# Four Strassen units in the last gate pair, its weights asked for behind x1's last read-back

## The chip, the cores and the metric

The kernel runs on one core of one Trainium2 chip. A core has TensorE (PE in the profile; PEld is its weight load), VectorE (DVE), ScalarE (ACT), GpSimd (POOL) and SyncE (SP), which here issues nearly all transfers between HBM and the on-chip memory. The metric is the device time of one execution in microseconds; the time of a kernel is the median of its runs.

## The reference

One layer of a hybrid decoder trunk for 256 tokens of width 2048. Cut to what matters:

```python
h = rmsnorm(x, norm_mix_g); u = h @ w_in          # split into branches and gates
...                                               
m = sigmoid(ga) * (ya @ w_a_out) + sigmoid(gb) * (yb @ w_b_out)
x = x + m @ w_o
gate = sigmoid(rmsnorm(x, ple_norm_g) @ w_ple_gate)
x = x + gate * (p @ w_ple_proj)
return rmsnorm(x, final_norm_g)
```

All of it is float32. The change lies in the product with `w_ple_gate` (2048 x 2048) and in what surrounds it; the sum `x + m @ w_o` is called x1 below.

## The kernel before

**Products.** Every matrix product with a weight is done as three products of a rounded type (FP32R), because each float32 operand is split into a high part and the rest: high times high, high times rest, rest times high. The weights come from HBM as float32 into one of three buffers of 1 MB each (`raw`, `load_raw`, lines 116 to 134). `split` (line 146) makes the two parts of a weight tile: ScalarE rounds it into `whi` (line 166), and VectorE subtracts that from the weights and writes `wlo` (line 167). These parts lie in ten buffers, six of a pool `late` and four of a pool `wp`, in this stage. TensorE then takes three matmuls per weight chunk of 128 rows and half of the tokens (lines 1269 and 1293).

**Steps, units, groups.** The work is a list `steps`; a group is one block of 512 output columns, or a pair of blocks, over all 2048 rows. Two or four steps make a unit, and a unit is one weight buffer of 1 MB. Most groups run their chunks one after the other (line 1269). A pair group follows a program of eight units (lines 41 to 47): `(0, c)` is a plain unit for the first block, two chunk pairs; `(1, c)` the same for the second; `(2, c)` a plain unit that takes the same rows for both blocks; `("S", c)` is a Strassen unit for one chunk pair c, which computes with 7 products of 128 x 512 what takes 8 (lines 1311 to 1321). A Strassen unit needs sums of weights: after its first split, `combine_weights` (lines 174 to 188) makes them on VectorE in place, with the operations of lines 184, 187 and 188. It has four splits, one of them of half the width, where a plain unit has two. It also needs sums of the other operand: `forms` (line 780) makes four of them, splits them and keeps them as `So0` and `So1`, for x1's first and second quarter.

**The end of the kernel.** The last groups are `w_o`'s blocks 2 and 3, the gate block 0 (`PG`, eight steps, positions `late` to `late + 7`), the gate pair 1 and 2 (`GP`, program `LATE`, from `late + 8` on) and the gate block 3 (the last group, lines 1460 to 1483). The pair's accumulators are eight: four in banks "g", one for each half of the tokens and each block, and four in banks "s" for Strassen products. `sums` (line 859) adds them up when they are complete: a copy on ScalarE (line 868), additions on VectorE (line 855), then the sigmoid (line 1025). The gate times the kept projection `p @ w_ple_proj`, added to x1, are the operations of lines 1028 and 1029 in `gated`; GpSimd multiplies with the final gain (line 1037). The last group runs in three passes, each in a bank: the first half of the tokens over 512 columns, then the second half over twice 256 columns. After each pass come the evictions of `last_half` and the norm.

**What sets the order.** The program is traced in the order of positions, and a scheduler of the compiler fixes each engine's order from that, from what it expects to be ready and from explicit ties: `tc.issue_after(i)` puts what is traced in the block behind instruction `i` on `i`'s engine, without a wait for its end. `step` ties the work after a product behind the splits traced last; `tied` is a list of ranges of positions whose splits are tied one behind the other. `ahead` (line 1257) says how many steps ahead of the products the splits are traced: three at `late`, eight from `late + 17` on. `ask_ahead` (line 1273) traces the weight loads up to two units further.

**Queues around the change.** x1 arrives in quarters of 512 columns. `turned` (line 338) transposes a quarter: four writes to HBM (line 350), one read back (line 354), then a transposition of small blocks on VectorE (line 358); `put` (lines 313 and 314) splits it into `xh` and `xl`. All these transfers, the weights (lines 119, 121, 126, 131) and the reads of the kept projections (`load_projection`, line 1220) stand in one queue of SyncE. The last quarter's transposition falls into the gate block 0, whose last two steps multiply with that quarter. In `load`, the weights of `w_o`'s plain blocks are tied behind the last of the four writes (`state["sent"]`).

Of the kernel before, what the change touches and what calls it, by code (L numbers as in the profile page):

```python
# [23 lines left out]
CW = 512  # L24
# [19 lines left out]
INNER = (0, 4), ("S", 0), (0, 6), ("S", 1), (2, 3), ("S", 2), (1, 4), (1, 6)  # L44
FRONT = (0, 2), (0, 4), (0, 6), ("S", 0), (1, 2), ("S", 1), (1, 4), (1, 6)
OUT = (0, 4), ("S", 0), (1, 4), ("S", 1), (2, 3), ("S", 2), (0, 6), (1, 6)
LATE = (0, 4), ("S", 0), (0, 6), ("S", 1), (2, 3), ("S", 2), (1, 4), (1, 6)


PRM_GMIX, PRM_GPLE, PRM_GHG, PRM_LB, PRM_CONV = 0, 16, 32, 40, 48  # L50
# [5 lines left out]
def hybrid_kernel(ctx, tc, xT, x, pT, prm, gfin, masks, w_in, w_a, w_b, w_o, w_pg, w_pp, out):  # L56
    nc = tc.nc
# [23 lines left out]
    state = {"tmp": "tmp1"}  # L81
# [3 lines left out]
    def nm(s):  # L85
        uid[0] += 1
        return f"{s}_{uid[0]}"

    def t4(tag="t4", bufs=None):
        bufs = bufs or {"tmp1": 8, "tmp2": 4, "tmp3": 5}[state["tmp"]]  # L90
        return pools[state["tmp"]].tile([P, 1024], F32, tag=tag, bufs=bufs, name=nm(tag))

    def bank(tag):
        return ps.tile([P, CW], F32, tag=tag, bufs=4, name=nm(tag))
# [7 lines left out]
    unit_of, part_of, joint, across = [], [], [], []  # L102
    loaded = {}
# [1 line left out]
    half = {}  # L105

    def load(pos):
        if unit_of[pos] not in loaded and groups[steps[pos][0]][0] == "O":
            with tc.issue_after(state["sent"]):
                return load_raw(pos)  # L110
        return load_raw(pos)

    def load_raw(pos):
        w, g, c = stream[pos]
        if unit_of[pos] not in loaded:
            raw = wp.tile([P, 2, 2 * CW], F32, tag="raw", bufs=3, name=nm("raw"))
            loaded[unit_of[pos]] = raw
            if joint[pos]:
                nc.sync.dma_start(out=raw[:, 0, :], in_=w[g, :, c, :])
                for i in range(2):  # L120
                    nc.sync.dma_start(
                        out=raw[:, 1, i * CW : (i + 1) * CW], in_=w[g + 1, :, c, (1 - i) * CW : (2 - i) * CW]
                    )
            elif across[pos]:
                for i in range(2):
                    nc.sync.dma_start(out=raw[:, i, :], in_=w[g + i, :, c, :])
            elif FIRST <= pos < FIRST + 20:
                for i in range(2):
                    nc.sync.dma_start(out=raw[:, i, :], in_=w[g, :, c + i, :])
            elif pos >= FIRST:  # L130
                nc.sync.dma_start(out=raw, in_=w[g, :, c : c + 2, :])
        return loaded[unit_of[pos]]
# [10 lines left out]
    def split(pos, c0=0, c1=2 * CW):  # L143
        part = part_of[pos]
        src = load(pos)[:, part % 2, :]
        if joint[pos]:

            src = load(pos)[:, part == 3, :]
            if part == 1:
                src, c1 = half[unit_of[pos]], CW  # L150

        pool, n = (pools["late"], 6) if (pos - state.get("late", len(steps))) % 10 < 6 and "late" in state else (wp, 4)
        places = [(pool, n, tag) for tag in ("whi", "wlo")]
        n = len(MORE[more(pos)])
        if pos % (4 + n) < n:
            places = [(pools[name], 1 + (tag == "X"), tag) for name, tag in MORE[more(pos)][pos % (4 + n)]]
        if pos not in parts:
            parts[pos] = tuple(
                pool.tile([P, 2 * CW << (tag[:3] == "yaT")], F32R, tag=tag, bufs=n, name=nm("w" + x))[:, : 2 * CW] for (pool, n, tag), x in zip(places, ("hi", "lo"))
            )  # L160
        hi, lo = parts[pos]
        s = slice(c0, c1)
        with ExitStack() as order:
            for i in (*(state["splits"] if more(pos) == "inner" or any(pos in at for at in tied) else ()),):
                order.enter_context(tc.issue_after(i))
            a = nc.scalar.activation(out=hi[:, s], in_=src[:, s], func=AF.Copy)  # L166
            v = nc.vector.tensor_tensor(  # L167
                out=lo[:, s], in0=src[:, s], in1=hi[:, s].bitcast(F32), op=ALU.subtract
            )
        state["splits"] = (a.ins, v.ins)  # L170
        if joint[pos] and part == 0:
            combine_weights(pos)
# [17 lines left out]
    groups = []  # L190
# [13 lines left out]
    groups += [("OO", 0, w_o, 0, "mT", OUT), ("O", 2, w_o, 2, "mT"), ("O", 3, w_o, 3, "mT")]  # L204
    groups += [("PG", 0, w_pg, 0, "x1T"), ("GP", 1, w_pg, 1, "x1T", LATE), ("PG", 3, w_pg, 3, "x1T")]
    steps = []
# [36 lines left out]
    gates, late = of_kind("GG"), of_kind("PG")[0]  # L243
# [6 lines left out]
    tied = []  # L250
# [4 lines left out]
    closing = last_unit("OO", OUT)  # L255
    last = range(gates[-1] + 1, closing + 1)
    outer = range(closing + 6, of_kind("O")[-1] + 1)
    tied.append(range(last[0] - 4, late + 10))
    inner = [of_kind(kind) for kind in ("QV", "VG")]
    inner = range(inner[0][0] - 3, inner[0][-1] + 1), range(inner[1][0] - 6, inner[1][-1] + 1)  # L260

# [79 lines left out]
    def turned(src, lag, dst=None):  # L341

        d = dram.tile([P, 4, T], F32, tag="turn", bufs=3, name=nm("turn"))
        to = d.rearrange("(b i) a x -> a i b x", b=4)
        for a in range(4):
            state["sent"] = nc.sync.dma_start(  # L350
                out=to[a], in_=src[32 * a : 32 * a + 32, :].rearrange("i (b x) -> i b x", b=4)
            ).ins
        yield
        nc.sync.dma_start(out=src, in_=d.rearrange("p a x -> p (a x)"))
        for _ in range(lag):
            yield
        dst = t4() if dst is None else dst
        nc.vector.transpose(
            out=dst.rearrange("p (k a e) -> p a k e", a=4, e=32), in_=src.rearrange("p (a k e) -> p a k e", a=4, e=32)
        )  # L360
        return dst
# [589 lines left out]
    def ep_o(j, psum):  # L951
# [18 lines left out]
        if j < 2:  # L970
# [6 lines left out]
            yield  # L977
            chunks = [c for u, c in LATE if u == "S" and c // 2 == j]
            r = x1.rearrange("p (u k t) -> p u k t", u=2, k=2)[:, : len(chunks)]
# [59 lines left out]
    def last_half(t, h, psum):  # L1039

        xs, pw, ss, n = state["x"], state["pw", 3], state["ss3"], CW // 2
        gt = t4()
        squares, gt = gt[:, : n + (t == 1 and h == 1)], gt[:, :n]
        d = xs[:, t, 3 * CW + h * n : 3 * CW + (h + 1) * n]
        nc.scalar.activation(out=gt, in_=psum, func=AF.Sigmoid, scale=state["rstd2"][:, t : t + 1])
        nc.vector.tensor_tensor(  # L1046
            out=gt, in0=gt, in1=pw[:, t * CW + h * n : t * CW + (h + 1) * n], op=ALU.mult
        )
        nc.vector.tensor_tensor(out=d, in0=d, in1=gt, op=ALU.add)
        if t == 1 and h == 1:  # L1050

            d = state["whole"][:, NT * D - n : NT * D + 1]
        nc.vector.scalar_tensor_tensor(
            out=squares, in0=d, scalar=1.0 / D, in1=d, op0=ALU.mult, op1=ALU.mult,
            accum_out=ss[:, t * 6 + 3 + h : t * 6 + 4 + h],
        )
# [47 lines left out]
    def ep_last(t, halves):  # L1104

        last_half(t, 0, halves[0])
        sums_so_far(t)
        last_half(t, 1, halves[1])
        last_norm(t)
        yield  # L1110
# [106 lines left out]
    def load_projection(j):  # L1217

        pw = state["pw", j] = t4("pw", 2)
        nc.sync.dma_start(out=pw, in_=state["kept", j])  # L1220

    def third_part():

# [25 lines left out]
    def advance():  # L1249
        for e in list(active):  # L1250
            step(e)
# [12 lines left out]
    def product(psum, op, k, t, hi, lo, first, last, which=(0, 1, 2)):  # L1264

        oh, ol = (x[:, k, t * P : (t + 1) * P] for x in op)
        for n in which:
            a, b = ((oh, hi), (oh, lo), (ol, hi))[n]
            m = nc.tensor.matmul(psum, a, b, start=first and n == 0, stop=last and n == 2)  # L1269
            if late + 5 <= pos < late + 12:  # L1270
                tc.keep_in_program_order(m)
# [62 lines left out]
    for pos, (gi, c) in enumerate(steps[:last_group]):  # L1334
# [85 lines left out]
        for i in range(2):  # L1420
            k = 2 * c + i
            for c0, c1 in EARLY[0][:2] if pos == 0 and i == 0 else ((0, CW),):
                s = slice(i * CW + c0, i * CW + c1)
# [35 lines left out]

    nlast = len(steps) - last_group  # L1460
    for t, halves in ((0, (0, 1)), (1, (0,)), (1, (1,))):
        bk, n = bank("g"), CW // 2
        for c in range(nlast):
            if done < len(steps):
                split(done)
                done += 1
            hi, lo = parts[last_group + c]
            for i in range(2):
                k = 2 * c + i
                s = slice(i * CW + halves[0] * n, i * CW + (halves[-1] + 1) * n)  # L1470
                product(bk[:, : len(halves) * n], state["x1T"], k, t, hi[:, s], lo[:, s], k == 0, k == KT - 1)
            if c % 2:
                advance()
        if t == 0:
            active.append(ep_last(t, [bk[:, h * n : (h + 1) * n] for h in halves]))
        else:
            last_half(t, halves[0], bk[:, :n])
            if halves[0] == 0:
                sums_so_far(t)
# [76 lines left out]
```

## Time and profile before

| | us |
|---|---|
| median of 3 runs | 807.52 (807.15 to 807.83) |
| the profiled execution | 807.97 |
| its span, from first to last instruction | 806.2 |
| TensorE busy | 797.0 |
| VectorE busy | 686.9 |
| ScalarE busy | 494.1 |
| GpSimd busy | 89.2 |

The profile is one execution. In a row of a timeline stand the start, the time, the engine, the line of the kernel, the operation, what is written and read, how many are merged, and in brackets the idle time of the engine before the row with what ended it. `SPq` rows are requests of SyncE's queue; their time is that of the request and not of the transfer. A matmul of 512 columns is shown with 0.39 us, but the next one starts 0.227 us later, since matmuls overlap. Likewise one VectorE split of 128 x 1024 is shown with 1.22 us and the next starts 1.14 us later.

### The profile page before, as it was taken

The numbers are of one execution on the slowest core, as the hardware profiler recorded it, in microseconds if no ns is written. First come the engines' busy times: TensorE is split into PE (matmuls) and PEld (weight loads), VectorE is DVE, ScalarE is ACT, GpSimd is POOL, SyncE is SP. The second block draws the span as 40 slices with busy tenths as digits, with TensorE's granted clock in tenths as the row PEclk, the third lists the DMA queues.
The fourth block names the chain that finished last, engine by engine and source line by source line (L and its number), as shares of the span: only waits on it lengthen the run. The fifth ranks groups of instructions, "written<-read, shape, count | busy, mean of one in ns | idle before, by whom it ended". The sixth has DMA issues, their size and how long they took to land.

```text
span 806.2 us, 11109 instructions
## 1 busy us (share of the span) xinstructions
PE 797.0 (99%) x4168; PEld 662.5 (82%) x4169; DVE 686.9 (85%) x794; ACT 494.1 (61%) x666; POOL 89.2 (11%) x74
## 2 busy tenths in 40 slices
PE   9999999999999999999999999999999999999995
PEld 7888888888888888888888888888888888888885
DVE  6969897966778987978998998998998998879894
ACT  7867575575665665586674564564565556765652
POOL 0000145300000054300001000100100000002012
PEclk9999999999999999999999999999999999999998
DMA  9899855747776755668584775775875669987532
GB/s 344 308 322 314 275 169 205 242 167 231 251 262 197 257 179 202 209 206 261 187 310 159 220 277 168 249 260 184 263 274 196 209 240 350 368 268 258 222 120 104
DMA packets 50309, 191.20 MB, mean 237 GB/s; under 512 B 5712, under 2 KB 15184, under 8 KB 36304
## 3 DMA queue, kind: packets, MB, share of 16 engines
q1 hardware_dynamic: 50112, 190.24, 68.7%
q8 instruction: 32, 0.52, 0.3%
q10 hardware_dynamic: 144, 0.26, 0.1%
q14 instruction: 21, 0.17, 0.1%
HBM read 175.80 MB, written 14.68 MB: 236 GB/s over the span
## 4 chain that ended last, share of the span: by engine, by line
PE 93%; DVE 3%; issue 1%; ACT 1%; DMA 1%; POOL 0%; ACTq 0%; POOLq 0%; DVEq 0%
PE g L1269 49%; PE g L1293 30%; PE s L1293 8%; PE s L1269 3%; DVE wlo L167 1%; PE s L514 1%; DMA raw<-in_w_pg 1%; PE s L1142 1%; DVE t L855 0%; DVE t L1028 0%; ACT whi L166 0%; DVE t L1046 0%; DVE xs L1029 0%; PE s L647 0%; PE s L670 0%
## 5 line engine op out<-in xcount | busy, mean ns | idle before, releaser
L167 DVE TENSOR_TENSOR wlo<-raw,whi 128x1024 fp32r<-128x1024 f32 (+1 forms) x320 | 392.2, 1249 | 85.0 <-ACT whi L166 83.6
L166 ACT ACTIVATE whi<-raw 128x1024 fp32r<-128x1024 f32 (+1 forms) x320 | 326.3, 1047 | 167.4 <-PE g L1269 93.4
L1269 PE MATMUL g<-whi,xh 128*128 128x512 f32 (+1 forms) x464 | 177.5, 383 | 0.0
L1269 PE MATMUL g<-whi,xl 128*128 128x512 f32 (+1 forms) x464 | 177.2, 382 | 0.0
L1269 PE MATMUL g<-wlo,xh 128*128 128x512 f32 (+1 forms) x464 | 177.1, 382 | 0.0
L1293 PE MATMUL g<-wlo,xh 128*128 128x512 f32 x316 | 122.9, 389 | 0.0
L1293 PE MATMUL g<-whi,xl 128*128 128x512 f32 x316 | 122.9, 389 | 0.0
L1293 PE MATMUL g<-whi,xh 128*128 128x512 f32 x316 | 122.4, 389 | 0.0
L1269 PEld LDWEIGHTS g<-whi,xh 128*128 128x128 f32 x464 | 87.2, 188 | 17.2 <-ACT xh L313 0.4
L1269 PEld LDWEIGHTS g<-whi,xl 128*128 128x128 f32 x464 | 87.2, 188 | 17.1 <-DVE xl L314 0.2
L1269 PEld LDWEIGHTS g<-wlo,xh 128*128 128x128 f32 x464 | 87.2, 188 | 16.6
L166 ACT ACTIVATE whi<-t 128x512 fp32r<-128x512 f32 x25 | 15.8, 632 | 91.3 <-DVE t L187 86.7
L1293 PEld LDWEIGHTS g<-wlo,xh 128*128 128x128 f32 x316 | 59.3, 188 | 12.4
L1293 PEld LDWEIGHTS g<-whi,xh 128*128 128x128 f32 x316 | 59.3, 188 | 12.3
L1293 PEld LDWEIGHTS g<-whi,xl 128*128 128x128 f32 x316 | 59.3, 188 | 12.2
L184 DVE TENSOR_TENSOR raw<-raw 128x1024 f32<-128x1024 f32 x25 | 31.5, 1262 | 0.7
L937 POOL TENSOR_TENSOR t<-ga,gb 128x512 f32<-128x512 f32 x6 | 10.6, 1788 | 188.0 <-issue 118.1
L1269 PE MATMUL g<-whi,yaTh 128*128 128x512 f32 (+1 forms) x74 | 28.3, 389 | 0.0
L1269 PE MATMUL g<-whi,yaTl 128*128 128x512 f32 (+1 forms) x74 | 28.0, 384 | 0.0
L1269 PE MATMUL g<-wlo,yaTh 128*128 128x512 f32 (+1 forms) x74 | 27.9, 383 | 0.0
L1269 PE MATMUL g<-whi,ybTh 128*128 128x512 f32 x64 | 24.9, 389 | 0.0
L1269 PE MATMUL g<-wlo,ybTh 128*128 128x512 f32 x64 | 24.9, 389 | 0.0
(317 smaller groups left out, 1110.6 us busy)
## 6 DMA issues: line engine op xcount, KB each, us to landing
raw<-in_w_in SPq DMA_DIRECT2D x68, 1024.0 KB, 5.0
raw<-in_w_in SPq DMA_DIRECT2D x37, 512.0 KB, 5.3
raw<-in_w_o SPq DMA_DIRECT2D x12, 1024.0 KB, 5.6
raw<-in_w_pg SPq DMA_DIRECT2D x12, 1024.0 KB, 6.5
raw<-in_w_in SPq DMA_DIRECT2D x38, 256.0 KB, 5.6
turn<-t SPq DMA_DIRECT2D x72, 128.0 KB, 2.8
t<-turn SPq DMA_DIRECT2D x18, 512.0 KB, 5.2
raw<-in_w_a SPq DMA_DIRECT2D x8, 1024.0 KB, 5.6
```

What stands on the lines that cost most here:

```text
L166: a = nc.scalar.activation(out=hi[:, s], in_=src[:, s], func=AF.Copy)
L167: v = nc.vector.tensor_tensor(out=lo[:, s], in0=src[:, s], in1=hi[:, s].bitcast(F32), op=ALU.subtract)
L184: nc.vector.tensor_tensor(out=b[:, 0:4:3, :], in0=b[:, 0:3:2, :], in1=b[:, 3:4, :].to_broadcast([P, 2, CW]), op=ALU.subtract)
L514: nc.tensor.matmul(heads(bk)[r, h, c if at is None else slice(at, at + 32)], key(h)[:, r], query(h)[:, c], start=True, stop=True, tile_pos ...
L937: (nc.vector if j == 3 else nc.gpsimd).tensor_tensor(out=spread(m, t), in0=blocks(ga[:, s]), in1=blocks(gb[:, s]), op=ALU.add)
L1142: nc.tensor.matmul(wb[:m, :n], *ones, start=True, stop=True)
L1269: m = nc.tensor.matmul(psum, a, b, start=first and n == 0, stop=last and n == 2)
L1293: m = nc.tensor.matmul(banks[name], x, y[:, s], start=k == total[name] and i == 0, stop=k == 1 and i == 2)
```

## The change

In the program of the last pair, the plain unit over both blocks for chunk 3 becomes a Strassen unit, and the plain unit of the second block goes ahead of the two Strassen units that now follow each other. The weight loads of the pair, save for its first unit at `late + 8`, are tied behind the read-back traced last, which for them is that of x1's last quarter; so are the reads of the kept projections. The range of tied splits reaches one position further, to the first split of the pair's first Strassen unit. The first pass of the last group takes a bank "s" instead of "g". Since chunk 3 lies in x1's second quarter, `forms` makes operands for two chunks there instead of one (line 978 takes them from `LATE`), and the pair has 24 steps instead of 22.

```diff
-LATE = (0, 4), ("S", 0), (0, 6), ("S", 1), (2, 3), ("S", 2), (1, 4), (1, 6)
+LATE = (0, 4), ("S", 0), (0, 6), ("S", 1), (1, 4), ("S", 2), ("S", 3), (1, 6)
...
     def load(pos):
-        if unit_of[pos] not in loaded and groups[steps[pos][0]][0] == "O":
-            with tc.issue_after(state["sent"]):
+        after = {"O": "sent", "GP": "read"}.get(groups[steps[pos][0]][0])
+        if unit_of[pos] not in loaded and after and pos != late + 8:
+            with tc.issue_after(state[after]):
                 return load_raw(pos)
         return load_raw(pos)
...
-    tied.append(range(last[0] - 4, late + 10))
+    tied.append(range(last[0] - 4, late + 11))
...
-        nc.sync.dma_start(out=src, in_=d.rearrange("p a x -> p (a x)"))
+        state["read"] = nc.sync.dma_start(out=src, in_=d.rearrange("p a x -> p (a x)")).ins
...
         pw = state["pw", j] = t4("pw", 2)
-        nc.sync.dma_start(out=pw, in_=state["kept", j])
+        with tc.issue_after(state["read"]):
+            nc.sync.dma_start(out=pw, in_=state["kept", j])
...
-        bk, n = bank("g"), CW // 2
+        bk, n = bank("g" if t else "s"), CW // 2
```

## Prediction

> **What bounds the kernel now.** I read the page first: TensorE is busy in 99% of the span, and 93% of the chain that ended last is TensorE. Then I read the chain in order of time around the last gate pair, where the change lies.
>
> ```profile
> span 806.2 us, 11109 instructions
> PE 93%; DVE 3%; issue 1%; ACT 1%; DMA 1%; POOL 0%; ACTq 0%; POOLq 0%; DVEq 0%
> ...
> 734.24 5.44 PE g L1293 x24
> ...
> 744.44 5.44 PE g L1293 x24
> ```
>
> A plain unit of the pair is 24 matmuls in 5.44 us, 0.2267 us each. From the first row to the second lie one plain and one Strassen unit, 10.20 us, so a Strassen unit (21 matmuls) takes 4.76. I looked along TensorE for starts further apart than 0.24 us after the opening and the attention products, and found one place:
>
> ```profile
> 728.08 0.39 PE L1269 MATMUL g<-whi,xl 128*128 128x512 f32 x1
> ...
> 729.30 0.40 PE L1269 MATMUL g<-whi,xh 128*128 128x512 f32 x1
> ```
>
> From the first row to the second are four starts, 1.22 us where 0.91 would do: 0.31 us lost, just when the first gate group reaches x1's last quarter. The three windows to the end show who stands next in line:
>
> ```profile
> 740.00:760.00 20.00, 20.00 (x90) 16.57 (x89) 19.23 (x19) 10.92 (x13) 4.77 (x2) 1.00 0.53 183
> 760.00:780.00 20.00, 20.00 (x90) 16.57 (x89) 18.22 (x19) 12.09 (x17) 1.45 (x2) 1.00 0.63 233
> 780.00:806.20 26.20, 18.11 (x126) 16.77 (x124) 15.74 (x37) 6.91 (x14) 5.74 (x6) 0.91 0.21 80
> ```
>
> Columns: length, PE, PEld, DVE, ACT, POOL, clock, DMA. VectorE is busy 19.23 and 18.22 of 20 us. TensorE sets the pace by a thin margin, and the change takes from TensorE and gives to VectorE.
>
> **What the change takes from TensorE.** One plain unit becomes a Strassen unit: three matmuls, 3 x 0.2267 = 0.68 us. The weights of the first Strassen unit are now asked for behind the read-back of x1's last quarter:
>
> ```profile
> 706.07 0.43 SPq L1220 DMA_DIRECT2D pw<-kept  x1
> 714.30 0.33 SPq L131 DMA_DIRECT2D raw<-in_w_pg  x1
> 715.98 2.31 SPq L350 DMA_DIRECT2D turn<-t  x4
> 718.39 0.57 SPq L119 DMA_DIRECT2D raw<-in_w_pg  x1
> 719.01 0.46 SPq L121 DMA_DIRECT2D raw<-in_w_pg  x1
> 721.77 0.33 SPq L354 DMA_DIRECT2D t<-turn  x1
> ...
> 724.89 1.23 DVE L167 TENSOR_TENSOR wlo<-raw,whi 128x1024 fp32r<-128x1024 f32 x1 [1.81 <-ACT whi L166]
> 726.60 1.25 DVE L358 STREAM_TRANSPOSE t<-t 128x1024 f32<-128x1024 f32 x1 [0.48 <-DMA t<-turn]
> 728.42 1.69 DVE L314 SCALAR_TENSOR_TENSOR xl<-t,prm_t,xh 128x256 fp32r<-128x256 f32 x4 [0.58 <-ACT xh L313]
> ...
> 736.62 1.28 DVE L1028 TENSOR_TENSOR t<-t,pw 128x512 f32<-128x512 f32 x2
> ```
>
> The two requests at 718.39 and 719.01 (768 KB) go behind 721.77, so the read-back, 4.8 us in flight today (721.77 to 726.60), finds less in its way. It has to win only 0.31 us to close the gap; bounds 0 and 0.31, and I take 0.31, since most of what is in front of it goes. The exempted unit (714.30) stays. Behind the read-back, which waits for its four writes, now stand the first Strassen unit's three requests besides those of the units after it; TensorE reaches that unit 5.44 us after 734.24, so the 3.7 us by which its first request moves cost TensorE nothing. The first read of the kept projection (706.07) is traced behind the first Strassen weights and moves to about 723.5. Two MB (read-back, weights, itself) then have to come from 721.77 on; at the 4.81 us per MB of the row at 758.68 below that is 731.4, and its first user comes at 736.62. Best case on TensorE: 0.99 us.
>
> **What it gives to VectorE.** (a) The first Strassen unit's first split ran at 724.89 in a gap. Its weights now come after the read-back, and the wider tied range puts it behind the preparation of x1 (the row at 728.42), into a stretch without gaps: +1.14, the step between splits in the row at 756.30 below ((4.63 - 1.22) / 3). The earlier read-back and the wait for ScalarE's half of that split, some tenths each, I let cancel. (b) The new unit costs a combine and four splits in place of two:
>
> ```profile
> 752.36 1.23 DVE L184 TENSOR_TENSOR raw<-raw 128x1024 f32<-128x1024 f32 x1
> ...
> 754.34 0.69 DVE L188 TENSOR_TENSOR raw<-raw,t 128x512 f32<-128x512 f32 x1
> 755.35 0.69 DVE L167 TENSOR_TENSOR wlo<-t,whi 128x512 fp32r<-128x512 f32 x1 [0.31 <-ACT whi L166]
> 756.30 4.63 DVE L167 TENSOR_TENSOR wlo<-raw,whi 128x1024 fp32r<-128x1024 f32 x4 [0.26 <-ACT whi L166]
> ...
> 758.68 4.81 DMA raw<-in_w_pg
> ...
> 763.60 2.01 ACT L166 ACTIVATE whi<-raw 128x1024 fp32r<-128x1024 f32 x2 [2.59 <-DMA raw<-in_w_pg]
> 764.69 2.36 DVE L167 TENSOR_TENSOR wlo<-raw,whi 128x1024 fp32r<-128x1024 f32 x2 [1.50 <-ACT whi L166]
> ```
>
> Combine 2.68 (752.36 to 755.04, where the wait of 0.31 begins), splits 3 x 1.14 + 0.69 = 4.11, less two plain splits, 2.28: +4.51. (c) There are three weight buffers. At 758.68 the third Strassen unit's last split freed one and a load of 4.81 us went into it. Two Strassen units in a row hold two buffers long: that split now ends at 758.66 + 1.14 - 0.57 (the two small gaps) = 759.2, the fourth unit is done 6.79 later at 766.0, and only then is the last group's second load asked for. It lands at 770.8 and ScalarE passes it on at 772.0. VectorE has by then done the plain unit and the first two splits of the last group (4 x 1.14, to 770.6): a new wait of 1.4, with bounds 0 and 2.8 (its double, if the next load too comes late). Sum (a) to (c): **7.05 us** more on VectorE.
>
> What covers it are VectorE's idle times up to the last evictions: 0.31, 0.26 and 1.50 above, and
>
> ```profile
> 775.56 0.69 DVE L1028 TENSOR_TENSOR t<-t,pw 128x512 f32<-128x512 f32 x1 [0.18 <-ACT t L1025]
> ...
> 779.01 3.44 DVE L167 TENSOR_TENSOR wlo<-raw,whi 128x1024 fp32r<-128x1024 f32 x2
> ...
> 783.84 1.31 DVE L1028 TENSOR_TENSOR t<-t,pw 128x512 f32<-128x512 f32 x2 [0.19 <-ACT t L1025]
> 787.51 2.08 DVE L1046 TENSOR_TENSOR t<-t,pw 128x256 f32<-128x256 f32 x2 [1.16 <-ACT t L1045]
> ...
> 798.65 0.43 DVE L1046 TENSOR_TENSOR t<-t,pw 128x256 f32<-128x256 f32 x1 [2.03 <-ACT t L1045]
> ```
>
> 0.18 + 0.19 + 1.16 + 2.03, in all 5.63. The last row waits for TensorE's end and opens the tail that ends the kernel. Uncovered: 7.05 - 5.63 = **1.42 us**; VectorE, not TensorE, would then release the tail, and the 0.99 won on TensorE lies behind it. The run of the profile took 807.97 (span 806.2 and 1.8 around it): 809.39 for that run. It stands 0.45 above the median of the runs, 807.52, so the forecast is **808.9**.
>
> At nothing I cost three things. ScalarE's two extra splits lie in its own waits (2.59 in the row at 763.60). The Strassen operands of x1's second quarter become twice as wide, four small operations of 0.28 and one of 0.68, at most 1.8 us more at 700 to 705, before a gap of 1.57:
>
> ```profile
> 700.73 0.28 DVE L787 SCALAR_TENSOR_TENSOR t<-t 128x128 f32<-128x128 f32 x1
> 703.81 0.68 DVE L795 TENSOR_TENSOR So1l<-t,So1h 128x512 fp32r<-128x512 f32 x1
> 710.61 1.22 DVE L167 TENSOR_TENSOR wlo<-raw,whi 128x1024 fp32r<-128x1024 f32 x1 [1.57 <-ACT whi L166]
> 765.51 0.58 ACT L868 ACTIVATE t<-s 128x512 f32<-128x512 f32 x1
> 775.56 0.39 PE L1269 MATMUL g<-whi,xh 128*128 128x512 f32 x1
> ```
>
> Of them 0.3 at most would be left, on VectorE alone. Third, the bank: the sums of the pair are traced behind the last group's fourth split (before: its second), so the copy at L868 moves to about 773.0 to 773.6. It frees the s bank 1.0 us before TensorE wants it (775.56 - 0.99 = 774.57). The g bank would come free with the first addition on VectorE, at 772.0 + 2.28 + 0.68 = 774.96, and cost 0.4.
>
> VectorE's operations also stretch where GpSimd works beside them:
>
> ```profile
> 741.42 2.19 DVE L184 TENSOR_TENSOR raw<-raw 128x1024 f32<-128x1024 f32 x1
> 739.40 5.37 POOL L1037 TENSOR_TENSOR xs<-xs,gfin_t 128x512 f32<-128x512 f32 x2 [15.54 <-ACT t L1030]
> ```
>
> 2.19 beside GpSimd against 1.23 without. The gain operations only move, so I count no change. The Trainium skill, "SBUF — State Buffer", section "Who interferes with whom", says that a VectorE instruction with two SBUF inputs contends with a GpSimd instruction that reads SBUF, and that the loser blocks for the whole instruction. By that rule, too, only the place of the loss changes: were the last split the victim of one more whole operation (5.37 / 2), the sum would be at most 2.7 us later. The trace shows both sides stretched rather than one blocked.
>
> **The rivals.** *All absorbed* (20%): the queue is put in a kinder order, VectorE catches up before the tail, TensorE keeps its 0.99: 807.52 - 0.99 = 806.5. For it: the idle 2.03 at the end; against: 19.23 busy of 20.
>
> *TensorE starved by the last split* (34%), the slower side: the last group's eighth split ended at 779.01 + 3.44 = 782.45, and TensorE wants it 7 steps of 6 matmuls after its start, now 774.57 + 9.52 = 784.1. Carried along with the ledger (7.05 less the 2.25 covered before it) it ends at 787.25, and TensorE waits 3.2 us: 2.2 net, 809.7. If the waits of 0.31, 0.26 and 1.50 move along instead of absorbing, another 2.07: 811.8. I take the middle, 810.7. It decides from the point where the split comes later than 784.1. Against it: it is now traced one step behind the gating of the first quarter instead of three, and if that gating (0.68 + 0.69 + 0.68 + 1.78 in today's order, some 3.8 us) falls behind it, it ends at 783.4 in time.
>
> *The ordering does nothing* (4%): the read-back is no faster, the gap of 0.31 stays; VectorE still ends the kernel, 808.9 to 809.1. *More than 0.2% faster* (4%): TensorE has no more than 0.99 to give, so it would need something that no row shows.
>
> **Chances.** About 0.2%, 1.6 us, is what a measurement can tell from no change: faster is below 805.9, slower above 809.1. The forecast case (VectorE's uncovered work ends the kernel, 807.9 to 809.6) has 38%, of which I put 9 above 809.1. Slower: 34 + 9 = 43%; same: 29 + 20 + 4 = 53%; faster: 4%. The range takes in the absorbed case and most of the starved one: 806.4 to 811.2; the forecast's own is 807.9 to 809.6.
>
> **What would show it.** Three matmuls fewer; no stretched starts near 728; the first Strassen requests behind the read-back; a VectorE wait of about 1.4 us for the last group's third split near 771; the idle before the last L1046 gone or nearly so. TensorE starts more than 0.3 us apart at 784 to 788 would show the starved case. I am wrong if VectorE still idles 1 us or more before that last L1046, and by more if TensorE waits inside the pair.

## The result, and the profile after

| | before | after |
|---|---|---|
| median (runs) | 807.65 (6) | **809.99** (6) |
| lowest to highest | 807.15 to 807.93 | 809.64 to 810.76 |
| profiled execution | 807.97 | 809.95 |
| its span | 806.2 | 808.2 |

The ratio of after to before is 1.0029, with a 95% interval of 1.0019 to 1.0039: slower by 2.3 us. That lies in the range (806.4 to 811.2) and beyond the forecast's own case (808.9; 807.9 to 809.6). By the prediction's line of 809.1 it is the slower case, which had 43%, where no change had 53%. What to learn here is which entries of the VectorE ledger were wrong.

From the page of the changed kernel, the span, the busy times and the chain that ended last by engine:

```profile
span 808.2 us, 11118 instructions
...
PE 796.5 (99%) x4165; PEld 662.0 (82%) x4166; DVE 690.6 (85%) x799; ACT 495.7 (61%) x668; POOL 90.9 (11%) x74
...
DVE 6%; issue 1%; ACT 1%; DMA 1%; POOL 0%; ACTq 0%; POOLq 0%; DVEq 0%
```

The matmuls are 4165 where there were 4168: three fewer, as the change asks. TensorE is busy 796.5 us instead of 797.0, and still the span grew by 2.0. The busy share hides it; the chain doesn't. It sums to some 9% of the span, since it could be followed back only to 730.05, the first split of the pair's first Strassen unit. From there to the end it holds no matmul, where 93% of the chain before was TensorE. Of its longest pieces these two lie where the ledger had its entries (c) and 1.16:

```profile
766.66 4.84 DMA raw<-in_w_pg
...
789.94 1.34 ACT t L1031 x4
```

The SyncE queue, with VectorE's transposition of x1's last quarter behind it and the first split and combine of the pair's first Strassen unit:

```profile
722.55 0.34 SPq L355 DMA_DIRECT2D t<-turn  x1
722.99 0.38 SPq L120 DMA_DIRECT2D raw<-in_w_pg  x1
723.41 0.90 SPq L122 DMA_DIRECT2D raw<-in_w_pg  x2
724.35 0.43 SPq L1222 DMA_DIRECT2D pw<-kept  x1
...
726.08 1.25 DVE L359 STREAM_TRANSPOSE t<-t 128x1024 f32<-128x1024 f32 x1 [2.08 <-DMA t<-turn]
...
730.05 1.23 DVE L168 TENSOR_TENSOR wlo<-raw,whi 128x1024 fp32r<-128x1024 f32 x1 [0.46 <-ACT whi L167]
731.31 1.23 DVE L185 TENSOR_TENSOR raw<-raw 128x1024 f32<-128x1024 f32 x1
```

The read-back is now ahead of the unit's requests, and it landed 0.52 earlier (726.08 against 726.60). VectorE, though, idled 2.08 us in front of it, the place where the first split used to stand. That split now comes at 730.05.

VectorE from there to the end, the rows that answer to those of before:

```profile
757.55 3.50 DVE L168 TENSOR_TENSOR wlo<-raw,whi 128x1024 fp32r<-128x1024 f32 x3 [0.48 <-ACT whi L167]
761.08 1.23 DVE L185 TENSOR_TENSOR raw<-raw 128x1024 f32<-128x1024 f32 x1
...
763.68 1.22 DVE L168 TENSOR_TENSOR wlo<-raw,whi 128x1024 fp32r<-128x1024 f32 x1
...
772.70 2.36 DVE L168 TENSOR_TENSOR wlo<-raw,whi 128x1024 fp32r<-128x1024 f32 x2 [1.53 <-ACT whi L167]
...
783.91 1.22 DVE L168 TENSOR_TENSOR wlo<-raw,whi 128x1024 fp32r<-128x1024 f32 x1
785.05 0.69 DVE L1030 TENSOR_TENSOR xs<-xs,t 128x512 f32<-128x512 f32 x1
...
787.14 2.16 DVE L1029 TENSOR_TENSOR t<-t,pw 128x512 f32<-128x512 f32 x2 [0.21 <-ACT t L1026]
789.22 1.28 DVE L1030 TENSOR_TENSOR xs<-xs,t 128x512 f32<-128x512 f32 x2
791.67 2.08 DVE L1047 TENSOR_TENSOR t<-t,pw 128x256 f32<-128x256 f32 x2 [1.17 <-ACT t L1046]
...
800.63 0.16 DVE L1075 TENSOR_TENSOR xs<-tot,tot 128x1 f32<-128x1 f32 x1 [0.73 <-POOL tot L1074]
800.70 0.42 DVE L1047 TENSOR_TENSOR t<-t,pw 128x256 f32<-128x256 f32 x1
```

The last gate's additions end at 790.50 (789.22 + 1.28), against 786.35 before (785.06 + 1.29): 4.15 late. The first-pass evictions begin at 791.67 against 787.51: 4.16 late. The idle time of 1.16 is there again, 1.17 long. The last eviction, which opens the tail, has no idle time any more: 800.70 against 798.65, **2.05 late**. From there to the end of the span both kernels take the same 7.5 us.

TensorE was starved once, by the last group's eighth split (783.91 to 785.13 above):

```profile
784.29 0.39 PE L1271 MATMUL s<-whi,xh 128*128 128x512 f32 x1
785.18 0.50 PE L1271 MATMUL s<-wlo,xh 128*128 128x512 f32 x1 [0.50 <-DVE wlo L168]
785.53 0.40 PE L1271 MATMUL s<-whi,xl 128*128 128x512 f32 x1
...
797.85 0.28 PE L1271 MATMUL g<-whi,xl 128*128 128x256 f32 x1
```

Starts 0.89 and 0.35 apart, where 0.23 would do, lose 0.8 us of the 0.99 that the change was to win on TensorE. Its last matmul starts at 797.85, as before (797.83). The experiments show that neither the gain nor the stall matters to the time of this kernel.

### The profile page after: what moved, and what is told of

It reads as the page before. It is cut to its first block, busy times and chain, and to the rows that moved or that the text cites. A ratio compares the mean times of both kernels' runs of the same rounds, so it can differ in the third digit from the quotient of the medians.

```text
span 808.2 us, 11118 instructions
## 1 busy us (share of the span) xinstructions
PE 796.5 (99%) x4165; PEld 662.0 (82%) x4166; DVE 690.6 (85%) x799; ACT 495.7 (61%) x668; POOL 90.9 (11%) x74
## 5 line engine op out<-in xcount | busy, mean ns | idle before, releaser
L1271 PE MATMUL g<-whi,xh 128*128 128x512 f32 (+1 forms) x448 | 171.2, 383 | 0.0
L1271 PE MATMUL g<-wlo,xh 128*128 128x512 f32 (+1 forms) x448 | 171.0, 382 | 0.0
L1271 PE MATMUL g<-whi,xl 128*128 128x512 f32 (+1 forms) x448 | 170.9, 382 | 0.0
L1295 PE MATMUL g<-wlo,xh 128*128 128x512 f32 x310 | 120.6, 389 | 0.0
L1295 PE MATMUL g<-whi,xl 128*128 128x512 f32 x310 | 120.6, 389 | 0.0
L1295 PE MATMUL g<-whi,xh 128*128 128x512 f32 x310 | 120.1, 389 | 0.0
L1271 PEld LDWEIGHTS g<-whi,xl 128*128 128x128 f32 x448 | 84.2, 188 | 16.4
L1271 PEld LDWEIGHTS g<-wlo,xh 128*128 128x128 f32 x448 | 84.2, 188 | 16.1
L1271 PEld LDWEIGHTS g<-whi,xh 128*128 128x128 f32 x448 | 84.2, 188 | 16.1
L1295 PEld LDWEIGHTS g<-whi,xl 128*128 128x128 f32 x310 | 58.2, 188 | 12.1
L1295 PEld LDWEIGHTS g<-wlo,xh 128*128 128x128 f32 x310 | 58.2, 188 | 12.1
L1295 PEld LDWEIGHTS g<-whi,xh 128*128 128x128 f32 x310 | 58.2, 188 | 12.1
```

The lines of the kernel that those rows point to most:

```text
L1295: m = nc.tensor.matmul(banks[name], x, y[:, s], start=k == total[name] and i == 0, stop=k == 1 and i == 2)
```

## The experiments

One measure is used for all of them: how long after the start of TensorE's last matmul the last eviction starts on VectorE. Where TensorE opens the tail this is 0.82 us. Where it is more, VectorE was late. Medians and ratios are against the kernel before, run in the same job (its medians there: 807.83, 807.74, 808.32 and 807.86).

| kernel | median | ratio, 95% interval | last matmul | last eviction | between |
|---|---|---|---|---|---|
| before | 807.65 | | 797.83 | 798.65 | 0.82 |
| after | 809.99 | 1.0029 (1.0019 to 1.0039) | 797.85 | 800.70 | 2.85 |
| e1 three Strassen units, new order | 807.55 | 0.9999 (0.9990 to 1.0008) | 797.63 | 798.45 | 0.82 |
| e2 no fourth combine | 806.91 | 0.9993 (0.9984 to 1.0002) | 796.85 | 797.83 | 0.98 |
| e3 first norm later | 808.35 | 1.0007 (0.9998 to 1.0015) | 798.48 | 799.66 | 1.18 |
| e4 other program | 806.94 | 0.9990 (0.9981 to 0.9998) | 796.24 | 797.06 | 0.82 |
| e5 four units, old order | 808.40 | 1.0007 (0.9998 to 1.0016) | 797.08 | 799.22 | 2.14 |
| e6 gate behind the split | 810.53 | 1.0033 (1.0021 to 1.0045) | 797.05 | 801.22 | 4.17 |
| e7 bank g | 809.25 | 1.0021 (1.0012 to 1.0029) | 799.69 | 802.25 | 2.56 |
| e8 e4 and e3 | 807.07 | 0.9995 (0.9984 to 1.0006) | 797.03 | 797.85 | 0.82 |
| e9 squares behind | 809.35 | 1.0012 (1.0003 to 1.0021) | 798.52 | 801.05 | 2.53 |
| e10 after again | 810.26 | 1.0024 (1.0015 to 1.0033) | 797.19 | 800.04 | 2.85 |
| e11 bank g again | 809.98 | 1.0020 (1.0011 to 1.0029) | 798.25 | 801.11 | 2.86 |
| e12 e9, no last gains | 808.13 | 1.0001 (0.9992 to 1.0010) | 798.07 | 798.89 | 0.82 |

A profile is one execution, and single runs of a kernel spread by up to 4 us here (e8: 806.42 to 810.56), so the last three columns are read within a row.

**The change taken apart: e1, e5, e2.** e1 keeps the ties and the bank and takes the fourth Strassen unit back:

```diff
-LATE = (0, 4), ("S", 0), (0, 6), ("S", 1), (1, 4), ("S", 2), ("S", 3), (1, 6)
+LATE = (0, 4), ("S", 0), (0, 6), ("S", 1), (2, 3), ("S", 2), (1, 4), (1, 6)
```

> The ties and the bank of the changed kernel, with the program of three Strassen units. VectorE theory: the first split of the first Strassen unit moves behind the preparation of x1 and puts VectorE 1.3 us later, which its idle time before 765 (0.31, 0.26, 1.50 us) takes up; TensorE loses its gap of 0.31 us near 728, nothing else: 0.3 us under the kernel before, so some 807.3. Rival 'the ordering does nothing': the gap stays and the time is that of before, 807.65. Rival 'the ordering alone makes the loss': the 1.3 us reach the end, 809 or more.

Measured 807.55, ratio 0.9999: the ties alone cost nothing here. The stretched starts near 728 are gone in its profile, but the 0.3 us that this may bring is less than the interval can tell from nothing. The expectation was wrong on why the time holds: VectorE's idle times didn't take up its delay. VectorE is 0.98 late at the first combine (731.00, before 730.02) and still 1.03 late after those idle times, which are there again (0.48 and 1.59). What gave the time back is told below, with the second step that failed. e5 is the other half, the kernel before with the new `LATE` and `bank("g" if t else "s")`, and no new ties:

> The program of four Strassen units and the bank of the changed kernel, without the ties: the first Strassen unit's weights and the kept projections are asked for as in the kernel before. VectorE theory: the first Strassen unit's first split goes back into the gap before x1's last quarter, VectorE's lag at the last pass falls from 4.2 us by some 1.2, and 0.9 of it stays uncovered by the 2.0 us before the last eviction: 808.7; the gap of 0.3 us on TensorE near 728 is back and costs nothing. Rival 'TensorE ends the kernel': the gap comes on top, 810.3. Rival 'the ties are neutral': 810.0.

Measured 808.40, near the 808.7 expected. The first split is back in the gap, the last split starves nobody (it ends at 783.66), and VectorE's last eviction still follows at once on its own work, at 799.22. TensorE loses 0.7 us near 728 in this profile, and that isn't what the end waits for. So neither half makes the loss alone: e1's ratio is that of no change, and so, within its interval, is e5's. VectorE's lag shows why. The last gate's additions end at 789.03 in e5, 2.68 late, and with the ties as well 4.15 late. The 2.03 that VectorE idled before the last eviction takes up most of the first and nothing of what the ties add. Together they take 809.99, 1.6 more than e5 (medians of different jobs), near the 1.47 that the ties add to the lag. e2 takes only the combine out of the changed kernel:

```diff
+        if pos == late + 26:
+            half[unit_of[pos]] = ...
+            nc.gpsimd.memset(half[unit_of[pos]], 0.0)
+            return
         combine_weights(pos)
```

> The changed kernel, with the three VectorE operations that sum the weights of the fourth Strassen unit left out (its half-width sum is filled with zeros by GpSimd, so the result of the pair is not the reference's). VectorE theory: 2.6 us less on VectorE before the last gates, so its lag of 4.2 us at the last pass falls to 1.5, under the 2.0 us that it idled before TensorE's end in the kernel before; the last split comes in time, TensorE keeps its 0.99 us and opens the tail again: 806.7 to 807.2. Rival 'TensorE starved by the last split sets the end': only its 0.8 us go, 809.2. Rival 'neither': 810.0 as the changed kernel.

Measured 806.91: three operations of VectorE, 2.6 us, are worth about 3 us of the kernel's time (809.99 less 806.91, across jobs). That is what a bound engine looks like.

**Does VectorE's tail or TensorE set the end: e3, e6.** e3 ties the scaling of the first half of the tokens behind the second pass's eviction, so that VectorE gets to the sum that opens the second norm earlier:

```diff
+        for i in state["evictions"] if t == 0 else ():
+            order.enter_context(tc.issue_after(i))
...
         last_half(t, 1, halves[1])
+        for _ in range(4):
+            yield
         last_norm(t)
```

> The changed kernel, with the scaling of the first half of the tokens (three VectorE operations of 1.3 us together and two of ScalarE) tied behind the eviction of the second pass; no operation is added or taken away and TensorE's order is the same. VectorE theory: the second pass's eviction, ready on TensorE at about 792.5, fills VectorE's and ScalarE's waits and the last eviction starts some 1.7 us earlier: 808.3. Rival 'TensorE starved sets the end': its last matmul does not move, 810.0.

Measured 808.35, although TensorE's last matmul starts later in its profile than in that of the changed kernel (798.48 against 797.85). Less work ahead of the last eviction on VectorE is what shortens the kernel. e6 does the reverse. It traces the pair's first gating one step behind the last split, so that TensorE isn't starved:

```diff
-            gate = gated(j + q, g, [g[:, A], g[:, B]])
-            next(gate)
-            active.append(gate)
...
+            active.append(gating())
+            if q:
+                next(active[-1])
```

> The changed kernel, with the gating of the pair's first quarter traced one step later, behind the last split of the last group. The same operations; TensorE's wait of 0.8 us at 784 goes. VectorE theory: VectorE has as much to do before the last eviction as in the changed kernel, so the time stays within 0.4 of 810.0 though TensorE ends 0.8 earlier. Rival 'TensorE starved sets the end': 809.2 or less.

Measured 810.53, far from the rival's 809.2 and just above the 0.4 around 810.0. The split ended at 782.07, TensorE ran without the stall at 784 and finished 0.80 earlier than in the changed kernel's profile, and nothing was gained: the stall costs nothing. VectorE even got later, its last eviction at 801.22 against 800.70. GpSimd and VectorE in that stretch of e6, a timeline each, show why:

```profile
786.47 3.30 POOL L1044 TENSOR_TENSOR xs<-xs,gfin_t 128x512 f32<-128x512 f32 x1 [40.37 <-ACT t L1037]
786.47 5.01 POOL L1044 TENSOR_TENSOR xs<-xs,gfin_t 128x512 f32<-128x512 f32 x2 [40.37 <-ACT t L1037]
789.73 3.19 POOL L1044 TENSOR_TENSOR xs<-xs,gfin_t 128x512 f32<-128x512 f32 x2
791.44 2.91 POOL L1044 TENSOR_TENSOR xs<-xs,gfin_t 128x512 f32<-128x512 f32 x2
```

```profile
788.65 1.67 DVE L1036 TENSOR_TENSOR xs<-xs,t 128x512 f32<-128x512 f32 x1
790.24 1.52 DVE L1053 TENSOR_TENSOR t<-t,pw 128x256 f32<-128x256 f32 x1
791.80 1.40 DVE L1056 TENSOR_TENSOR xs<-xs,t 128x256 f32<-128x256 f32 x1
793.23 1.41 DVE L1060 SCALAR_TENSOR_TENSOR t<-xs 128x256 f32<-128x256 f32 x1
```

The four rows of GpSimd overlap and cover four operations in a row, which end at 789.77, 791.48, 792.92 and 794.35. VectorE's four end at 790.32, 791.76, 793.20 and 794.64, each 0.3 to 0.55 behind one of GpSimd's: about its own length. Each waits for the whole of GpSimd's operation and then runs, and loses about 1 us.

**The bank: e7, e11.** `bank("g")` for all three passes:

> The changed kernel with the last group's first pass in a bank g. That bank comes free with VectorE's first addition (775.7 in the changed kernel's trace), 0.9 us after TensorE wants it. VectorE theory: TensorE waits there instead of at the last split, whose wait shrinks by as much, and VectorE still ends the kernel: 810.0. Rival 'each of TensorE's waits counts': 810.9.

e7 came out at 809.25, lower than either theory had it. It was run again beside the changed kernel (e10):

> The changed kernel as it is, beside the two others of this job: 809.6 to 810.4, and with it the difference of each of the others is read on one chip. In its trace, the starts of TensorE near 728 show how far the landing of x1's last read-back varies from run to run (bounds from the runs so far: 0 and 1.1 us lost).

> The changed kernel with the last group's first pass in a bank g again, now beside the changed kernel. Before, its time was 809.25, 0.7 below the 809.99 of the changed kernel in another job, though TensorE waited about 1.3 us for that bank at 776. If the bank costs nothing because VectorE sets the end, the two are within 0.4 of each other here. If the wait for the bank itself helps (TensorE's and VectorE's work come in a kinder order), it stays 0.5 or more below; if that wait counts, it is 0.9 or more above.

809.98 for bank g and 810.26 for the changed kernel on the same chip: no difference, and the 0.7 of e7 was one of jobs. In e11's TensorE timeline the bank is late:

```profile
774.65 0.39 PE L1295 MATMUL g<-whi,xl 128*128 128x512 f32 x1
775.77 0.50 PE L1271 MATMUL g<-whi,xh 128*128 128x512 f32 x1 [0.74 <-DVE t L856]
776.11 0.39 PE L1271 MATMUL g<-wlo,xh 128*128 128x512 f32 x1
```

TensorE loses 1.0 us here (starts 1.12 and 0.34 apart), more than the 0.4 I gave it, and the time is the same: once VectorE sets the end, the bank costs nothing.

**What the idle time of 1.17 is: e9, e12.** e9 puts ScalarE's two squares of the last gate behind the two evictions of the first pass. GpSimd's two gains of that gate stay behind the squares, and the sums of the first half go behind both evictions:

```diff
+                with tc.issue_after(state["eviction"]):
+                    nc.scalar.activation(
+                        out=junk[:, s], in_=xs[:, t, j * CW : (j + 1) * CW], func=AF.Square,
...
+            state["behind"] = squares, gain
...
         last_half(t, 0, halves[0])
-        sums_so_far(t)
         last_half(t, 1, halves[1])
+        for work in state["behind"]:
+            work()
+        sums_so_far(t)
```

> The changed kernel, but ScalarE's two squares of the last gate (L1031, 789.94 and 790.57 in its profile) are put behind the two evictions of the first pass on ScalarE (L1046, 791.18); nothing else moves. Theory: the 1.17 us that VectorE idles before its first-pass evictions (L1047 at 791.67) isn't slack. The pass is complete on TensorE at 786.6, but ScalarE takes its evictions behind those squares, which wait for VectorE's own last addition (790.50), so the idle time travels with VectorE's work. With the squares behind, the evictions are done at about 788.6, VectorE goes on at 790.5 without a pause, the last eviction comes 1.0 to 1.2 earlier, at about 799.6, and the time is 808.8 to 809.0 (1.0 to 1.2 below the changed kernel run beside it). Rival: the evictions wait for something else (the bank, the transfer of the projection, TensorE); then 0.8 us or more of idle stays there and the time stays within 0.4 of the changed kernel.

The time was 809.35, 0.9 below the changed kernel in the same job, just short of the theory, but the intervals overlap. The trace is clearer than the time. VectorE in e9, from the last gate's additions to the sum that opens the first norm:

```profile
789.90 1.28 DVE L1030 TENSOR_TENSOR xs<-xs,t 128x512 f32<-128x512 f32 x2
791.10 0.75 DVE L1067 TENSOR_TENSOR t<-t,pw 128x256 f32<-128x256 f32 x2
791.77 2.94 DVE L1070 TENSOR_TENSOR xs<-xs,t 128x256 f32<-128x256 f32 x2
...
795.78 0.16 DVE L1101 TENSOR_TENSOR tot<-tot,ss 128x1 f32<-128x1 f32 x1
```

The idle time is gone, and the two additions behind the evictions take 2.94 instead of 0.75: GpSimd's last two gains, which start 0.2 us after VectorE's last gate addition in both kernels (791.41 here), now hold up these two for 2.19 us. In the changed kernel they cost the two evictions 1.33 (2.08 at 791.67, against 0.75 here). From 791.18 to 795.78 go 4.60 us, against 4.91 in the changed kernel (790.50 to 795.41). So neither verdict of the expectation fits: the idle time was ScalarE's order, as the theory had it, but behind it stood GpSimd. e12 keeps e9's order and leaves out GpSimd's two gains:

```diff
-            state["behind"] = squares, gain
+            state["behind"] = squares,
```

> As e9 (ScalarE's squares of the last gate behind the first pass's evictions), and GpSimd's two multiplications of the last gate's block with the final gain (L1038 in the changed kernel, L1050 in e9) are left out. In e9 the idle time ahead of VectorE's first-pass evictions went, but one of the two additions behind them took 2.19 us longer beside GpSimd (2.94 for two, 0.75 without), so that from the last gate's addition (end 791.18) to the sum that opens the first norm (795.78) 4.60 us went by, against 4.91 in the changed kernel. Theory: those 4.9 us are the delay of ScalarE's order and of GpSimd together, either of which fills the place of the other. Without both, the stretch is 2.3 to 2.6, VectorE ends the first half of the tokens early enough for TensorE to open the tail again as in the kernel before (last eviction at 798.5 to 798.9, after an idle time of VectorE of 0.1 to 0.6), and the time is 807.8 to 808.5. Rival: the stretch doesn't shrink below 4 us, VectorE still opens the tail, and the time is 809.2 or more.

```profile
789.43 1.28 DVE L1030 TENSOR_TENSOR xs<-xs,t 128x512 f32<-128x512 f32 x2
790.63 0.75 DVE L1067 TENSOR_TENSOR t<-t,pw 128x256 f32<-128x256 f32 x2
791.31 0.75 DVE L1070 TENSOR_TENSOR xs<-xs,t 128x256 f32<-128x256 f32 x2
...
793.11 0.16 DVE L1101 TENSOR_TENSOR tot<-tot,ss 128x1 f32<-128x1 f32 x1
...
798.89 0.42 DVE L1067 TENSOR_TENSOR t<-t,pw 128x256 f32<-128x256 f32 x1 [0.42 <-ACT t L1064]
```

Now the stretch is 2.40 (790.71 to 793.11), VectorE waits for TensorE again at the end, and the time is 808.13, ratio 1.0001. The loss of the change is gone with 2.5 us of waiting removed from this one stretch. As the gains are left out, this is a measurement and no version to use.

**A better program: e4, e8.** e4 gives the pair another order and leaves the rest of the change:

```diff
-LATE = (0, 4), ("S", 0), (0, 6), ("S", 1), (1, 4), ("S", 2), ("S", 3), (1, 6)
+LATE = ("S", 0), (0, 4), ("S", 1), (0, 6), ("S", 2), (1, 4), ("S", 3), (1, 6)
```

> The changed kernel with the program S0, plain, S1, plain, S2, plain, S3, plain: the same units, no two Strassen units in a row, the first one at the exempted position. VectorE theory: the first unit's combine and first splits, 3.7 us, fall into VectorE's gaps before x1's last quarter (0.6 and 2.1 us near 721 and 724) and the wait of 1.5 us for the last group's third split goes; the lag at the end falls from 4.2 to about 1: TensorE ends the kernel, 806.7. Rival: the first Strassen unit's weights now delay x1's last quarter on VectorE, or come too late for TensorE at 734: more than 808.

Measured 806.94, ratio 0.9990 with an interval that ends at 0.9998: the fourth Strassen unit, with plain units between, is faster than the changed kernel by some 3 us (across jobs), and than the kernel before by 0.9, less than what a measurement surely tells from no change. VectorE of e4 around the landing of x1's last quarter, at the last group's third split and at the end:

```profile
722.36 1.23 DVE L185 TENSOR_TENSOR raw<-raw 128x1024 f32<-128x1024 f32 x1 [1.35 <-DMA raw<-in_w_pg]
...
725.07 0.69 DVE L168 TENSOR_TENSOR wlo<-t,whi 128x512 fp32r<-128x512 f32 x1
725.68 1.24 DVE L359 STREAM_TRANSPOSE t<-t 128x1024 f32<-128x1024 f32 x1
...
768.90 2.36 DVE L168 TENSOR_TENSOR wlo<-raw,whi 128x1024 fp32r<-128x1024 f32 x2 [1.51 <-ACT whi L167]
...
796.81 0.16 DVE L1075 TENSOR_TENSOR xs<-tot,tot 128x1 f32<-128x1 f32 x1 [0.73 <-POOL tot L1074]
797.06 0.42 DVE L1047 TENSOR_TENSOR t<-t,pw 128x256 f32<-128x256 f32 x1
```

The first unit of the program is exempt from the tie. Here that is a Strassen unit, so its whole combine (722.36 to 725.07) fills the gap in which VectorE of the changed kernel idles 2.08, and the unit's first split is done before it. That accounts for nearly the whole difference: the last gate's additions end at 786.68, 0.33 late instead of 4.15, and combine and split are some 3.7 us. The other half of the expectation failed, since the wait for the last group's third split stands, 1.51 long, though no two Strassen units follow each other. VectorE reaches the last eviction just as TensorE ends: 0.09 us lie between the two last rows (796.81 + 0.16 to 797.06). e8 adds e3's edit to e4:

> The interleaved program together with the later scaling of the first half of the tokens. VectorE theory: with the interleaved program TensorE's end opens the tail, VectorE being ready at about the same time; relieving VectorE by 1.7 us more brings nothing or a tenth: 806.8 to 807.0. Rival 'VectorE still ends it there': up to 1.7 us less, 805.3.

Measured 807.07: nothing more. In its profile VectorE idles 1.62 ahead of the last eviction; TensorE opens the tail, and relieving VectorE there wins nothing more.

## Why the prediction was right, and where it wasn't

**The mechanism was right.** TensorE lost its three matmuls, VectorE came to set the end, the idle time of 2.03 before the last eviction went, and the wait of the last group's third split is there: 1.53 at 772.70, forecast 1.4 near 771. The reason given for that wait was wrong, as the cover below shows.

**TensorE.** No start near 728 is stretched in the profile of after, as forecast. This isn't certain from run to run: of the ten profiles with the ties and the pair's first unit as in the changed kernel, five lose nothing at that place and five lose 0.3 to 1.1 us (1.1 in e9, 0.5 in e12). The stall at 784 is the rival's, and smaller than the rival had it (0.8 instead of 3.2). It lies behind VectorE, as e6 showed, so the rival gives the wrong reason for a time near its own.

**VectorE's additions were nearly right in size.** (a) forecast 1.14; the first combine came at 731.31, against 730.02 before: 1.29. (b) the combine was forecast at 2.68 and took 2.60 (761.08 to 763.68). (c) 1.53 for 1.4.

**The step that failed is the cover**: "What covers it are VectorE's idle times up to the last evictions", in all 5.63. I took every idle time of VectorE as room. Of these 2.03 was room, and was used whole; 0.18 went. The others are round trips: VectorE waits for something that had itself waited for VectorE.

The 1.50 is one, and (c) is the same wait again. The last Strassen unit's last split frees a weight buffer, the next load goes into it, ScalarE takes its half of the split, and VectorE has four splits to do meanwhile. In the kernel before, that split ends at 758.66, the load is asked for at 758.68 and the wait, there at the last group's first split, is 1.50; in the changed kernel it is 766.64, 766.66 and 1.53. The wait is there with three Strassen units (e1, 1.59) and with four that lie apart (e4, 1.51), so it doesn't take two in a row. The prediction took 1.50 as cover and added 1.40 as a new wait, and these two errors all but cancel.

The rest goes by way of ScalarE alone. Where 0.31 and 0.26 stood there is 0.48 now, behind the combine that ScalarE's split needs; for 0.19 there is 0.21, behind VectorE's own sums; for 1.16 there is 1.17. The last, by rows of ScalarE in the changed kernel:

```profile
789.94 0.64 ACT L1031 ACTIVATE t<-xs 128x512 f32<-128x512 f32 x1 [2.22 <-DVE xs L1030]
...
790.57 0.62 ACT L1031 ACTIVATE t<-xs 128x512 f32<-128x512 f32 x1
...
791.18 0.82 ACT L1046 ACTIVATE t<-s,r2r 128x256 f32<-128x256 f32 x2
```

ScalarE idles 2.22 us, squares what VectorE has just added, and only then takes the evictions that VectorE waits for, though the pass had been complete on TensorE since 786.6. An idle time like this moves with the late engine.

**A second step failed the other way**: "The gain operations only move, so I count no change". The two gains of the pair's first block held VectorE twice in the kernel before. Its rows of GpSimd and VectorE there:

```profile
777.17 1.37 POOL L1037 TENSOR_TENSOR xs<-xs,gfin_t 128x512 f32<-128x512 f32 x1 [32.40 <-ACT t L1030]
779.92 1.45 POOL L1037 TENSOR_TENSOR xs<-xs,gfin_t 128x512 f32<-128x512 f32 x1 [1.38 <-ACT t L1030]
...
777.30 1.78 DVE L1029 TENSOR_TENSOR xs<-xs,t 128x512 f32<-128x512 f32 x1
```

The addition took 1.78 against 0.69 without GpSimd (785.05 above), and the two splits of the row at 779.01 took 3.44 against 2.36 (772.70 above): in all 2.17 lost. In the changed kernel the first of them came while VectorE's split and addition were running (783.91, 785.05) and waited itself:

```profile
784.23 3.92 POOL L1038 TENSOR_TENSOR xs<-xs,gfin_t 128x512 f32<-128x512 f32 x2 [38.16 <-ACT t L1031]
```

3.92 for two on GpSimd, against 1.37 and 1.45 before. VectorE lost only once, at 787.14: 2.16 for two against 1.28, 0.88. That gave 1.29 back. In e1 the same thing repaid the moved first split: VectorE is 1.03 late at the first split of its last group (765.72, before 764.69) and 0.42 early at the last additions (784.64, before 785.06).

**The ledger with what was measured.** To the end of the last gate's additions I had 4.61 late: 7.05 less the covers up to there, 2.44. With (a) +0.15, the combine -0.08, GpSimd -1.29 and the idle times +0.82 (2.22 are left, 0.48 + 1.53 + 0.21, where I had the 1.40 of (c) alone) it is 4.21; measured 4.15. Then nothing of 1.16, all of 2.03: about 2.1 late, measured 2.05, where I had 1.42. Cover that wasn't there (0.82 + 1.16) and a loss beside GpSimd that wasn't repeated (1.29) partly cancel; the remaining 0.6 is the distance of the profiled run (809.95) to my 809.39 for it. That the forecast missed by only 1.1 us is in part luck. The medians add some tenths of their own (2.34 between them against 1.98 between the profiles).

**The bank** was put down with 0.4 for g; TensorE lost 1.0 in e11, and the time nothing.

**The rule of the Trainium skill** that I weighed ("SBUF — State Buffer", section "Who interferes with whom"), that the loser of the two engines blocks for the whole instruction, holds; for VectorE instructions with two SBUF inputs the same page has it in its section "Summary: rules for kernel authors". I wrote that the traces show both sides stretched rather than one blocked. Both are stretched, but in turn: e6's rows show each VectorE operation ending about its own length after GpSimd's. The section on who interferes also says that issue order decides who blocks, and the trace agrees: GpSimd's gain at 784.23 came second and waited, and in e9 VectorE's addition at 791.77 came behind GpSimd's gain at 791.41 and waited. By that rule the change did alter the sum, since it altered the order.

## What to carry to other kernels

Before counting an engine's idle time as room for more work, follow its releasers back, through transfers too: if one of them had waited for this engine, the idle time is a round trip and moves along. Of the 5.63 counted here only 0.18 and the 2.03, which TensorE ended on its own, absorbed anything. When work is given to an engine that is nearly full, put it into one of its gaps by the order of the program (e4: the first split and combine ahead of x1's last quarter); the same fourth unit made this kernel 2.3 us slower in one place and no slower in another. And a removed idle time can be filled at once by the next wait behind it, as GpSimd's gains did in e9; leaving both out for one run tells what they cost together.

## What the runs showed that was not expected

The read-back of x1's last quarter is in flight 4.8 us in the kernel before and 3.3 to 3.8 in the ten profiles with the ties in which VectorE waited for it (722.04 to 725.44 in e10, 722.55 to 726.08 in after, 721.93 to 725.77 in e1). But its request, which waits for four writes, comes anywhere between 721.9 and 723.9 in these runs of nearly the same program, and TensorE loses between nothing and 1.1 us there. e5, without ties, had 3.9 in its one profile (722.59 to 726.51), so how much of the faster transfer the ties bring isn't settled by single profiles.
